# Full-height transpositions and products for the probabilities of a streaming encoder step, with a tile of its own for the prefix

## The chip, the core and the metric

The kernel runs on one core of one Trainium2 chip. The metric is the device time of one execution in microseconds (us), as the median of several runs. A core has five engines that run beside each other: TensorE (PE in the profile, with its weight loads shown apart as PEld), VectorE (DVE), ScalarE (ACT), GpSimd (POOL) and SyncE (SP). Each takes its own instructions in its own order; semaphores make one engine wait for another. DMAs are issued from an engine's queue, here from SP, and at a few places from ACT and POOL.

## The reference, cut to what matters

One layer of an encoder for 16 meta tokens and 512 prompt frames, and for 64 sample frames with 128 cached rows. Two groups of eight heads share one input projection: differential attention (two softmaxes, the second subtracted with a factor) and latent attention. Their outputs are joined and projected; a feed-forward part follows.

```
s   = einsum('bqhcd,bkhcd->bhcqk', qd, kd) * DIFF_SCALE + bias
p   = softmax(where(visible, s, neg))
p   = p[:, :, 0] - lam * p[:, :, 1]
o_d = einsum('bhqk,bkhe->bqhe', p, vd)
...
sm  = (einsum('bqhd,bkhd->bhqk', qn, km) + einsum('bqhr,bkr->bhqk', qr, krope)) * MLA_SCALE
pm  = softmax(where(visible, sm, neg))
o_m = einsum('bhqk,bkhe->bqhe', pm, vm)
```

The change touches only how `p` times the values is computed, in both groups: 16 heads in all.

## The kernel before

Matrices are held as two parts, high and low, and a product is made of three matmuls (high by high, high by low, low by high) in a 4-byte type. TensorE's order is the program's order: a small scheduler (`Streams`) interleaves generators, one for each strand of work, by estimated times, and every matmul and transposition is pinned in the order in which it was recorded. The other engines' orders are made when the program is built, from what each instruction needs.

From about 85 to 520 us the kernel projects the inputs (`project`, tile `ps`, weights `wr` split into `wh` and `wl`) and between these matmuls runs the eight differential heads (`diff_attend`). From about 520 to 785 us it runs the eight latent heads (`latent_attend`) between the matmuls of the output projection (`mix_out`, also `ps`). From there on is the feed-forward part, which the change doesn't touch.

For a head the softmax of a block of 128 queries (b = 0 to 3) is written to `pt_b[b]`, with one row for each query and one column for each key. The 64 sample queries go to `p5`. `probabilities_times_values` then works in groups g = 0 to 3. In each it turns blocks of probabilities with TensorE into the PSUM tile `tp` (L114 in the profile), ACT and DVE copy `tp` into the high and low part of `pk`, and matmuls multiply `pk` by the values into `po` (L110). Group g's matmuls (`last()`) are issued behind the transpositions of group g + 1.

Three places work with fewer than 128 rows:

- **The prefix.** The 16 meta tokens are keys of every block. To multiply high and low parts in one matmul, the three parts of their values lie stacked in rows 64 to 111 of slice 4 of `vh`; rows 0 to 63 of that slice hold the values of the 64 sample frames. For the probabilities, GpSimd copies the 16 meta columns of `pt_b[b]` three times behind its last column (`thrice`, L307, tile `p` in the profile). Group 1 transposes 112 columns of each `pt_b[b]`: the last 64 keys, which are not used, and the 48 copies. ACT copies rows 64 to 111 of `tp`, and `times_meta` multiplies 48 rows of `pk` by 48 rows of `vh`, over 512 columns, behind the transpositions of group 2.
- **The sample's probabilities.** `p5` has 64 rows. Groups 2 and 3 end with a transposition of it over 64 rows, against a 64 x 64 part of the identity.
- **The sample's products.** At the end, the tile `po5` (named `po` in the trace) gets two matmuls over 128 rows (cached values, slice 5), and two over 64 rows (own values, slice 4). The last latent head has three and three.

In the profile a TensorE row shows first the rows and columns of the stationary operand, then the rows and columns of the moving one: `48*128 48x512` is a product over 48 rows, with 512 columns streamed.

The lines of `probabilities_times_values` at these places:

```python
PE.transpose(tp[:, 384:384 + NS], p5[:, c:c + P], ident[0:NS, 0:NS])          # groups 2 and 3
PE.transpose(tp[0:STACK, b * P:(b + 1) * P], pt_b[b][:, w - NS:w + 3 * NM], ident)   # group 1
PE.matmul(po, vh[NS:STACK, 4, :], pk[NS:STACK, 1, :], start=False, stop=False)   # times_meta
```

Here NM = 16, NS = 64, STACK = 112 and P = 128.

In the latent half two heads are under way at a time, each with its own `pt_b` and `p5` (`probs[0]` for even heads, `probs[1]` for odd ones). The values of a pair of heads, `vh` and `vl`, have one buffer. When the last head's softmax is done, `tail` issues ten loads from POOL's queue: four pieces of `w_out` (`raw`, L1306) and six stored head outputs (`ml`, L1304). They are the operands of the output projection of the latent heads, the matmuls `ps<-mh,...` that begin at about 765 us.

Of the kernel before, what the change touches and what calls it, by code (L numbers as in the profile page):

```python
# [11 lines left out]
F32 = mybir.dt.float32  # L12
# [121 lines left out]
def encoder_step(  # L134
# [25 lines left out]
    def f32(ap):  # L160
        return ap.bitcast(F32)
# [65 lines left out]

    def probabilities_times_values(pt_b, p5, own0, past0, vh, vl, pool, tbanks, pso, pace, done, add=None,
                                   own_bank=True):
# [8 lines left out]
        def times_meta(pk):  # L238
            PE.matmul(po, vh[NS:STACK, 4, :], pk[NS:STACK, 1, :], start=False, stop=False)

# [8 lines left out]
        for g, blocks in enumerate((((0, 0), (0, 1), (0, 2), (0, 3)), (), ((1, 1), (1, 2), (1, 3)),  # L249
                                    ((2, 2), (2, 3), (3, 3)))):  # L250
            if g:
                yield pace
            bank, tbank = tbanks[g % len(tbanks)]
            yield from st.take(bank)
            tp = tbank()
            pk = pair(g)
            for n, (t, b) in enumerate(blocks):
                PE.transpose(tp[:, n * P:(n + 1) * P], pt_b[b][:, NM + t * P:NM + (t + 1) * P], ident)
            if g > 1:
                c = (past0, own0)[g - 2]  # L260
                PE.transpose(tp[:, 384:384 + NS], p5[:, c:c + P], ident[0:NS, 0:NS])
                kept.append(pk[:, :, 384:384 + NS])
            if g != 1:
                w = 448 if g else 512
                split(pk[:, 1, 0:w], pk[:, 0, 0:w], tp[:, 0:w])
            else:
                for b in range(4):
                    w = NM + P * (b + 1)
                    PE.transpose(tp[0:STACK, b * P:(b + 1) * P], pt_b[b][:, w - NS:w + 3 * NM], ident)
                S.activation(pk[NS:STACK, 1, :], tp[NS:STACK, :], AF.Copy)  # L270
                sub_lo(pk[96:STACK, 1, :], tp[96:STACK, :], pk[96:STACK, 1, :])
            last()
# [17 lines left out]
        if add:  # L290
            both_parts = po5[:, 0:2 * NS].rearrange("p (a b) -> p a b", a=2)
            PE.matmul(both_parts, vh[:, 5, :], kept[0], start=True, stop=False)
            PE.matmul(po5[:, NS:2 * NS], vl[:, 5, :], ph, start=False, stop=False)
            PE.matmul(po5[:, NS:2 * NS], vl[0:NS, 4, :], sh[0:NS], start=False, stop=False)
            PE.matmul(both_parts, vh[0:NS, 4, :], kept[1][0:NS], start=False, stop=True)
            done(po5[:, NS:2 * NS], SEQ, TQ)
            add(po5[:, 0:NS])
        else:
            todo = [(v[:, 5, :], p) for v, p in ((vh, ph), (vh, pl), (vl, ph))]
            todo += [(v[0:NS, 4, :], p[0:NS]) for v, p in ((vh, sh), (vh, sl), (vl, sh))]  # L300
            for n, (a, b) in enumerate(todo):
# [4 lines left out]
    def thrice(t, c0, n, copy):  # L306
        copy(t[:, n:n + 3 * NM].rearrange("p (r c) -> p r c", r=3),  # L307
             t[:, c0:c0 + NM].unsqueeze(1).to_broadcast([P, 3, NM]))
# [75 lines left out]
    with ExitStack() as ph:  # L384
# [268 lines left out]

        def keys_room(tag, name):
            return kv.tile([P, 6 * P], F32R, name=name, tag=tag, bufs=2)

        def values_room(tag, name, dtype=F32R):
            return kv.tile([P, 6, P], dtype, name=name, tag=tag, bufs=2)
# [6 lines left out]
        pt_b = [ap.tile([P, P * (b + 1) + 4 * NM], F32, name=f"p{b}") for b in range(4)]  # L665
        p5 = ap.tile([NS, NS + P], F32, name="p5")

# [62 lines left out]
        def diff_attend(h, khs, kl, vh, vl):  # L730
# [8 lines left out]
            for b in range(5):  # L739
# [3 lines left out]
                for c in range(2):  # L743
# [18 lines left out]
                    if c == 0:  # L762
# [14 lines left out]
            yield from probabilities_times_values(  # L777
                pt_b, p5, 0, NS, vh, vl, ap, [("tp", tbank)], pso, 1.0,
                lambda po, lo_, hi_: S.activation(o32[:, lo_:hi_], po, AF.Copy),
# [74 lines left out]
        def projections():  # L854
            for h in range(H):
# [34 lines left out]
                V.tensor_tensor(hv(z), ev(ps), hv(rb), op=ALU.mult)  # L890
                thrice(z, 0, T, lambda o, i: S.activation(o, i, AF.Copy))
# [4 lines left out]
                vh, vl = values_room("vh", "vh"), values_room("vl", "vl")  # L896
                nat[2 * h + 1] = st.spawn(0, values(h, z, vh, vl))
                att[h] = st.spawn(1, diff_attend(h, khs, kl, vh, vl),
# [37 lines left out]
        def query_latent(i, z):  # L936
            cqh[i], cql[i] = (zl.tile([P, TQ], F32R, name=f"cq{w}{i}", tag=f"q{i // 2}{i % 2}{t}")
                              for w, t in zip("hl", "sz"))
            if i == 0:
                sqs[0] = values_room("vl", "sqs", F32).rearrange("p a b -> p (a b)")[:, 0:TQ]  # L940
                S.activation(sqs[0], z, AF.Square)
# [63 lines left out]
        def latent_keys():  # L1005
# [4 lines left out]
            ch.extend([keys_room("kh0", "ch0"), keys_room("kh1", "ch1")])  # L1010
            cl.extend([keys_room("kl", "cl0"), values_room("vh", "cl1").rearrange("p a b -> p (a b)")])
            rk.extend([rkh, rkl])
# [7 lines left out]
            for i in range(2):  # L1020
                split(ch[i][:, 0:PROMPT], cl[i][:, 0:PROMPT], zs[4 + i][:, 0:PROMPT])
                split(ch[i][:, OWN_K:TP], cl[i][:, OWN_K:TP], zs[4 + i][:, PROMPT:T])
                split(*[x[i][:, TP:TP + 3 * NM].rearrange("p (r c) -> p r c", r=3) for x in (ch, cl)],
                      zs[4 + i][:, 0:NM].unsqueeze(1).to_broadcast([P, 3, NM]))
# [36 lines left out]
        named = dict(done=False)  # L1061
        aq, probs = [], []

        def latent_room():
# [5 lines left out]
            for i in range(2):  # L1070
                pb = [aq[0].tile([P, P * (b + 1) + 4 * NM], F32, name=f"p{b}{i}") for b in range(4)]
                p5 = aq[0].tile([NS, 2 * P], F32, name=f"p5{i}")
                G.memset(p5[:, NS + P:2 * P], 0.0)
                probs.append((pb, p5))
            for i, tag in enumerate(("vl", "vh", "vl")):
                km_rooms.append(values_room(tag, f"km{i}").rearrange("p a b -> p (a b)")[:, 0:TP])
            km_rooms.append(aq[0].tile([P, TP], F32R, name="km3"))
# [82 lines left out]
        def pair_values(j):  # L1160

            wh, wl = weights4(w_ukv4[:, :, 2 * j:2 * j + 2, 128:256], [P, 2, 2, P])
            vh = aq[0].tile([P, 6, 2 * P], F32R, name="vh")
            vl = aq[0].tile([P, 6, 2 * P], F32R, name="vl")
            for i, (o, n) in enumerate([(NM + P * j, P) for j in range(4)] + [(OWN_K, STACK), (PROMPT, PAST)]):
                yield from st.take("tp")
# [32 lines left out]
        def latent_attend(h, qn, km):  # L1199
            i = h % 2  # L1200
            pb, p5 = probs[i]
            yield 2.0
            for b in range(5):
# [9 lines left out]
                V.reciprocal(ls[0:n], ls[0:n])  # L1213
                dst = p5[:, 0:W] if b == 4 else pb[b][:, 0:W]
                V.tensor_scalar(dst, e[0:n, 0:W], ls[0:n], None, op0=ALU.mult)
                if b < 4:
                    thrice(pb[b], 0, W, G.tensor_copy)
                st.give(bank, 1.2 + 0.002 * W)
                yield 1.0
            asked[h]["done"] = True  # L1220
            yield [valued[h // 2]] + ([lat[h - 1]] if h else [])
            yield 1.5
            vh, vl = valued[h // 2]["v"]
# [5 lines left out]
            else:  # L1229
# [3 lines left out]
            yield from probabilities_times_values(  # L1233
                pb, p5, P, 0, vh[:, :, c], vl[:, :, c], aq[0], tbanks, pso, 1.0 * (h == H - 1), done, add,
                own_bank=h < H - 1)
# [866 lines left out]
```

## Time and profile before

| What | Value |
|---|---|
| Median of 3 runs | 2387.44 us (2387.34 to 2389.55) |
| Profiled execution | 2385.59 us, of which the profile's span is 2383.8 us |
| Granted TensorE clock in the profiled execution | 0.999 |
| DVE, ACT, POOL busy | 75%, 49%, 31% of the span |
| DMA | 340.92 MB moved, 143 GB/s on the mean |

The profile's busy shares are of one execution. TensorE's matmuls are pipelined, and their ends in the trace are modelled, so that the distance from one start to the next tells more than a duration. Where the trace's timeline merges equal instructions, the row has the start of the first, the time from there to the end of the last, and the count.

### The profile page before, as it was taken

The page shows a single profiled execution, that of the slowest core. Times are in us where ns is not written, and L with a number is a line of the kernel's source. Part 1 is how long each engine was busy: PE and PEld are TensorE (multiplying, and loading weights), DVE is VectorE, ACT ScalarE, POOL GpSimd, SP SyncE. Part 2 cuts the span into 40 slices and gives each one's busy share as a digit, 9 for nine tenths or more (in the row PEclk, how much of TensorE's full clock was granted, in tenths as well). Part 3 has the DMA queues.
Part 4 walks back from the last instruction along what each step waited for, and adds up shares of the span by engine and source line. Part 5 has one row for each costly group of instructions (what it writes and reads, how often), then busy time and mean ns, then how long its engine had stood idle before and what let it go on. Part 6 is the DMA issues. An engine that isn't in the chain of part 4 may idle for free.

```text
span 2383.8 us, 44654 instructions
## 1 busy us (share of the span) xinstructions
PE 2351.1 (99%) x17496; PEld 2317.2 (97%) x17496; DVE 1796.5 (75%) x2893; ACT 1163.7 (49%) x2259; POOL 727.8 (31%) x606
## 2 busy tenths in 40 slices
PE   9999999999999999999999999999999999999998
PEld 8999999999998999999999999999999999999998
DVE  6665666776665788788888888888888887877984
ACT  5554455454454554445545555555555433333444
POOL 1000000020001454554454454554554322222320
PEclk9999999999999999999999999999999999999999
DMA  9433333353323553334434434434434975655432
GB/s 286 122 90 87 86 91 92 94 162 107 95 93 126 158 163 109 127 112 150 160 115 149 161 116 147 161 119 144 161 120 149 326 258 167 228 166 169 156 103 98
DMA packets 330547, 340.92 MB, mean 143 GB/s; under 512 B 22610, under 2 KB 272376, under 8 KB 330304
## 3 DMA queue, kind: packets, MB, share of 16 engines
q1 hardware_dynamic: 328720, 334.30, 43.3%
q8 instruction: 137, 2.24, 0.4%
q0 software_dynamic: 1104, 3.22, 0.4%
q10 hardware_dynamic: 512, 0.55, 0.1%
q14 instruction: 74, 0.61, 0.1%
HBM read 267.21 MB, written 74.15 MB: 143 GB/s over the span
## 4 chain that ended last, share of the span: by engine, by line
PE 88%; DVE 5%; DMA 2%; ACT 2%; issue 2%; POOL 0%; SPq 0%; ACTq 0%; DVEq 0%; POOLq 0%
PE m L1494 38%; PE m L1498 19%; PE ps L110 19%; PE m L196 2%; PE sp L110 2%; PE po L110 2%; DVE wl L127 1%; PE tp L114 1%; PE m L1900 1%; PE pv L110 1%; PE pso L110 1%; ACT wh L127 0%; DMA wr<-in_w_in 0%; PE psv L110 0%; SPq L127 0%
## 5 line engine op out<-in xcount | busy, mean ns | idle before, releaser
L1494 PE MATMUL m<-b,wh 128*128 128x288 f32 x7168 | 1051.2, 296 | 4.5 <-DVE b L127 1.5
L1494 PEld LDWEIGHTS m<-b,wh 128*128 128x128 f32 x7168 | 982.8, 188 | 8.3 <-issue 3.3
L1498 PE MATMUL m<-b,wl 128*128 128x288 f32 x3584 | 570.0, 294 | 2.8 <-DVE wl L127 2.6
L1454 POOL TENSOR_TENSOR ws<-raw 128x512 f32<-128x512 f32 (+1 forms) x258 | 368.6, 1437 | 540.1 <-DVE wl L127 269.6
L1498 PEld LDWEIGHTS m<-b,wl 128*128 128x128 f32 x3584 | 509.1, 188 | 4.5 <-DVE wl L127 4.4
L127 ACT ACTIVATE wh<-ws 128x512 fp32r<-128x512 f32 (+1 forms) x339 | 282.9, 845 | 393.4 <-PE m L1494 245.7
L127 DVE TENSOR_TENSOR wl<-ws,wh 128x512 fp32r<-128x512 f32 (+1 forms) x339 | 379.7, 1128 | 95.4 <-ACT wh L127 92.5
L127 DVE TENSOR_TENSOR wl<-raw,wh 128x512 fp32r<-128x512 f32 (+1 forms) x393 | 367.5, 959 | 14.1 <-ACT wh L127 11.0
L127 ACT ACTIVATE wh<-raw 128x512 fp32r<-128x512 f32 (+1 forms) x393 | 231.1, 620 | 287.8 <-PE m L1494 233.3
L110 PE MATMUL ps<-xh,wh 128*128 128x296 f32 (+1 forms) x960 | 217.3, 307 | 0.5 <-ACT xh L127 0.5
L110 PE MATMUL ps<-xl,wh 128*128 128x296 f32 (+1 forms) x960 | 207.8, 298 | 0.4 <-DVE xl L127 0.3
L110 PE MATMUL ps<-xh,wl 128*128 128x296 f32 (+1 forms) x928 | 200.8, 297 | 0.5 <-DVE wl L127 0.5
L307 POOL COPY p<-p 128x48 f32<-128x48 f32 x64 | 20.2, 316 | 542.6 <-DVE p L127 500.4
L127 DVE TENSOR_TENSOR y<-y,m 128x288 f32<-128x288 f32 x280 | 125.9, 450 | 59.0 <-PE m L1498 58.8
L127 DVE TENSOR_TENSOR ws<-ws,raw 128x512 f32<-128x512 f32 (+1 forms) x129 | 112.6, 878 | 68.7 <-POOL ws L1454 66.6
L110 PEld LDWEIGHTS ps<-xh,wh 128*128 128x128 f32 x960 | 154.5, 189 | 5.6 <-issue 1.9
L110 PEld LDWEIGHTS ps<-xl,wh 128*128 128x128 f32 x960 | 154.9, 188 | 0.9 <-DVE xl L127 0.9
L110 PEld LDWEIGHTS ps<-xh,wl 128*128 128x128 f32 x928 | 150.2, 188 | 0.7 <-DVE wl L127 0.7
L127 DVE TENSOR_TENSOR wl<-wr,wh 128x1024 fp32r<-128x1024 f32 (+1 forms) x106 | 111.3, 1050 | 29.8 <-ACT wh L127 28.3
L127 ACT ACTIVATE wh<-wr 128x1024 fp32r<-128x1024 f32 (+1 forms) x108 | 97.5, 903 | 65.1 <-PE ps L110 37.3
L1719 POOL TENSOR_TENSOR c<-c,rb 128x576 f32<-128x576 f32 x42 | 67.2, 1600 | 168.4 <-ACT c L127 168.4
L127 ACT ACTIVATE parts<-c 128x1 fp32r<-128x1 f32 (+1 forms) x266 | 85.7, 322 | 33.5 <-DVE c L127 26.2
(396 smaller groups left out, 3103.6 us busy)
## 6 DMA issues: line engine op xcount, KB each, us to landing
raw<-in_ffn_w_gate SPq DMA_DIRECT2D x44, 1024.0 KB, 6.0
raw<-in_ffn_w_up SPq DMA_DIRECT2D x44, 1024.0 KB, 6.4
raw<-in_ffn_w_down SPq DMA_DIRECT2D x39, 1024.0 KB, 5.9
partspill<-parts SPq DMA_DIRECT2D x133, 288.0 KB, 2.1
b<-partspill SPq DMA_DIRECT2D x133, 288.0 KB, 6.2
wr<-in_w_in SPq DMA_DIRECT2D x54, 512.0 KB, 3.8
wr<-in_w_out SPq DMA_DIRECT2D x16, 512.0 KB, 4.1
wr<-in_w_out SPq DMA_DIRECT2D x24, 256.0 KB, 3.3
```

What stands on the lines that cost most here:

```text
L110: self.tc.keep_in_program_order(self.pe.matmul(out, lhsT, rhs, start=start, stop=stop))
L114: self.tc.keep_in_program_order(self.pe.transpose(out, in_, identity))
L127: ins = issue(*args, **kwargs)
L196: PE.matmul(outs[i], w, x[i], start=start and p == 0, stop=stop and p == 2)
L307: copy(t[:, n:n + 3 * NM].rearrange("p (r c) -> p r c", r=3), t[:, c0:c0 + NM].unsqueeze(1).to_broadcast([P, 3, NM]))
L1454: engine.tensor_tensor(w[:, k:k + m, :], pick(xs), pick(ys), op=op)
L1494: PE.matmul(banks[p], wh[k], x, start=first and new and k == 0 and x is hi, stop=False, skip_group_check=not new)
L1498: PE.matmul(banks[p], wl[k], hi, start=False, stop=last and k == n - 1, skip_group_check=not new)
L1719: engine.tensor_tensor(g[:, f, :], g[:, f, :], rb2, op=ALU.mult)
L1900: PE.matmul(bank[:, c0:c0 + 256], a[:, o:o + n], b, start=k + i == 0, stop=k == len(acts) - 1 and i == 2)
```

## The change

Every transposition and product of the three places gets 128 rows; the rows that are added hold zeros.

- The three copies of the meta columns go to a tile `pm` of their own (128 x 4 x 128, columns 64 to 111 of each block), which is set to zero once by POOL. Group 1 transposes `pm[:, b, :]`, all 128 columns, and ACT evicts all 128 rows. `pt_b` loses its 48 extra columns.
- `p5` gets 128 rows and 256 columns, zeroed once: columns 0 to 127 for the cached keys, 128 to 191 for the own ones. Its transpositions run over 128 rows against the whole identity, and stream 128 columns instead of 64. In the differential heads the write to `p5` becomes two instructions on DVE.
- Rows 96 to 127 of slice 4 of `vh` and rows 64 to 127 of slice 4 of `vl` are zeroed by POOL for each differential head and each pair of latent heads (`clear_rest`). The products on slice 4 take all 128 rows.
- In the latent half there is one `pm` for both sets of probabilities. So the copies into it are recorded not within the softmax loop, but behind it and behind the wait for the head before (`lat[h - 1]`).

The core of the diff:

```diff
         def times_meta(pk):
-            PE.matmul(po, vh[NS:STACK, 4, :], pk[NS:STACK, 1, :], start=False, stop=False)
+            PE.matmul(po, vh[:, 4, :], pk[:, 1, :], start=False, stop=False)
...
             if g > 1:
-                c = (past0, own0)[g - 2]
-                PE.transpose(tp[:, 384:384 + NS], p5[:, c:c + P], ident[0:NS, 0:NS])
+                PE.transpose(tp[:, 384:512], p5[:, (g - 2) * P:(g - 1) * P], ident)
...
                 for b in range(4):
-                    w = NM + P * (b + 1)
-                    PE.transpose(tp[0:STACK, b * P:(b + 1) * P], pt_b[b][:, w - NS:w + 3 * NM], ident)
-                S.activation(pk[NS:STACK, 1, :], tp[NS:STACK, :], AF.Copy)
-                sub_lo(pk[96:STACK, 1, :], tp[96:STACK, :], pk[96:STACK, 1, :])
+                    PE.transpose(tp[:, b * P:(b + 1) * P], pm[:, b, :], ident)
+                S.activation(pk[:, 1, :], tp, AF.Copy)
+                sub_lo(pk[96:P, 1, :], tp[96:P, :], pk[96:P, 1, :])
...
-            PE.matmul(po5[:, NS:2 * NS], vl[0:NS, 4, :], sh[0:NS], start=False, stop=False)
-            PE.matmul(both_parts, vh[0:NS, 4, :], kept[1][0:NS], start=False, stop=True)
+            PE.matmul(po5[:, NS:2 * NS], vl[:, 4, :], sh, start=False, stop=False)
+            PE.matmul(both_parts, vh[:, 4, :], kept[1], start=False, stop=True)
...
-            todo += [(v[0:NS, 4, :], p[0:NS]) for v, p in ((vh, sh), (vh, sl), (vl, sh))]
+            todo += [(v[:, 4, :], p) for v, p in ((vh, sh), (vh, sl), (vl, sh))]
...
+    def clear_rest(vh, vl):
+        G.memset(f32(vh[96:P]), 0.0)
+        G.memset(f32(vl[NS:P]), 0.0)
...
+        def probability_tiles(pool, i=""):
+            pt_b = [pool.tile([P, P * (b + 1) + NM], F32, name=f"p{b}{i}") for b in range(4)]
+            p5 = pool.tile([P, 2 * P], F32, name=f"p5{i}")
+            G.memset(p5, 0.0)
+            return pt_b, p5
+
+        def prefix_tile(pool):
+            pm = pool.tile([P, 4, P], F32, name="pm")
+            G.memset(pm, 0.0)
+            return pm
...
-                dst = p5 if b == 4 else pt_b[b][:, 0:W]
-                V.scalar_tensor_tensor(dst, es[0][0:n, 0:W], ls[0:n, 0:1], es[1][0:n, 0:W],
-                                       op0=ALU.mult, op1=ALU.subtract)
+                for dst, k in [(pt_b[b][:, 0:W], slice(0, W))] if b < 4 else [
+                        (p5[0:NS, P:P + NS], slice(0, NS)), (p5[0:NS, 0:P], slice(NS, W))]:
+                    V.scalar_tensor_tensor(dst, es[0][0:n, k], ls[0:n, 0:1], es[1][0:n, k],
+                                           op0=ALU.mult, op1=ALU.subtract)
                 if b < 4:
-                    thrice(pt_b[b], 0, W, G.tensor_copy)
+                    repeat(pm[:, b, NS:NS + 3 * NM], pt_b[b][:, 0:NM], G.tensor_copy)
...
             asked[h]["done"] = True
             yield [valued[h // 2]] + ([lat[h - 1]] if h else [])
+            for b in range(4):
+                repeat(pm[:, b, NS:NS + 3 * NM], pb[b][:, 0:NM], G.tensor_copy)
             yield 1.5
```

The remaining lines rename rooms and pass `pm` along. `repeat` is `thrice` with its destination given.

TensorE's order doesn't change: instruction stands beside instruction, only the shapes differ. Here is a piece of the difference on PE in the first differential head, group 2: the transpositions of `pt_b[2]` and `pt_b[3]` (`p_909`, `p_910`), that of `p5` (`p_911`), and the product with the prefix behind it. Printed is the shape of the result, which doesn't show the rows that are summed over.

```order
 L114 MATMUL tp<-ident,p_909 128x128
 L114 MATMUL tp<-ident,p_910 128x128
-L114 MATMUL tp<-ident,p_911 128x64
-L110 MATMUL po<-pk_1570,vh 128x512
+L114 MATMUL tp<-ident,p_911 128x128
+L110 MATMUL po<-pk_1578,vh 128x512
 L110 MATMUL ps<-xh_116,wh 128x288 x2
```

Nothing has moved there: the transposition of `p5` writes 128 columns in place of 64, and the product stands where it stood.

GpSimd's order does change in the latent half. Here is POOL at the end of it, before: the four copies of the last head (`p_6120` to `p_6123`), then the loads that `tail` issues (`raw`, `ml`).

```order
L307 COPY p_6120<-p_6120 128x48
L307 COPY p_6121<-p_6121 128x48
L307 COPY p_6122<-p_6122 128x48
L307 COPY p_6123<-p_6123 128x48
L1306 DMA raw<-in_w_out 128x4x128 x4
L1304 DMA ml_9034<-mspill_78 128x576
```

And the same place in the changed kernel, with the last copy of head 6 (`p_6144`) and the four of head 7 (`p_6147` to `p_6150`):

```order
L315 MEMSET vh 32x256
L306 COPY pm<-p_6144 128x48
L306 COPY pm<-p_6147 128x48
L306 COPY pm<-p_6148 128x48
L306 COPY pm<-p_6149 128x48
L306 COPY pm<-p_6150 128x48
L1323 DMA raw<-in_w_out 128x4x128 x4
L1321 DMA ml_9071<-mspill_78 128x576
```

The order of names is the same, but the four copies of head 7 now write the one `pm`. So each of them waits until the transposition of the same block of head 6 has read it, and the ten loads stand behind them.

More of the change, by code (lines that the diff above doesn't have):

```diff
@@ L226, in project_stacked, with probabilities_times_values @@
                 yield 0
-    def probabilities_times_values(pt_b, p5, own0, past0, vh, vl, pool, tbanks, pso, pace, done, add=None,
+    def probabilities_times_values(pt_b, pm, p5, vh, vl, pool, tbanks, pso, pace, done, add=None,
                                    own_bank=True):
@@ L304, in probabilities_times_values, with repeat @@
         st.give("po", 1.0)
-    def thrice(t, c0, n, copy):
-        copy(t[:, n:n + 3 * NM].rearrange("p (r c) -> p r c", r=3),
-             t[:, c0:c0 + NM].unsqueeze(1).to_broadcast([P, 3, NM]))
+    def repeat(dst, src, copy):
+        n = dst.shape[1] // NM
+        copy(dst.rearrange("p (r c) -> p r c", r=n), src.unsqueeze(1).to_broadcast([P, n, NM]))
     def stacked_values(vh, vl, src):
@@ L652, in encoder_step, with flat_room, values_room @@
         zk = zk_cm.__enter__()
[L654 to L658, printed above, removed]
+        ROOM = TP + 3 * NM
+        def flat_room(tag, name, dtype=F32R):
+            return kv.tile([P, ROOM], dtype, name=name, tag=tag, bufs=2)
+        keys_room = flat_room
+        def values_room(tag, name):
+            return flat_room(tag, name)[:, 0:6 * P].rearrange("p (a b) -> p a b", a=6)
         qs = [[[zl.tile([P, TQ], F32R, name=f"q{i}{c}{s}", tag=f"q{i}{c}{s}") for s in "sz"] for c in range(2)]
@@ L664, in encoder_step @@
                 G.memset(f32(qs[i][c][1][both[1 - c], :]), 0.0)
-        pt_b = [ap.tile([P, P * (b + 1) + 4 * NM], F32, name=f"p{b}") for b in range(4)]
-        p5 = ap.tile([NS, NS + P], F32, name="p5")
+        def probability_tiles(pool, i=""):
[7 more added lines that the diff above has]
+            return pm
+        (pt_b, p5), pm = probability_tiles(ap), prefix_tile(ap)
         def natural(src32, c0, rest, dst_p, stores, keep):
@@ L777, in diff_attend @@
             yield from probabilities_times_values(
-                pt_b, p5, 0, NS, vh, vl, ap, [("tp", tbank)], pso, 1.0,
+                pt_b, pm, p5, vh, vl, ap, [("tp", tbank)], pso, 1.0,
                 lambda po, lo_, hi_: S.activation(o32[:, lo_:hi_], po, AF.Copy),
@@ L890, in projections @@
                 V.tensor_tensor(hv(z), ev(ps), hv(rb), op=ALU.mult)
-                thrice(z, 0, T, lambda o, i: S.activation(o, i, AF.Copy))
+                repeat(z[:, T:T + 3 * NM], z[:, 0:NM], lambda o, i: S.activation(o, i, AF.Copy))
                 if h == 0:
@@ L896, in projections @@
                 vh, vl = values_room("vh", "vh"), values_room("vl", "vl")
+                clear_rest(vh[:, 4, :], vl[:, 4, :])
                 nat[2 * h + 1] = st.spawn(0, values(h, z, vh, vl))
@@ L939, in query_latent @@
             if i == 0:
-                sqs[0] = values_room("vl", "sqs", F32).rearrange("p a b -> p (a b)")[:, 0:TQ]
+                sqs[0] = flat_room("vl", "sqs", F32)[:, 0:TQ]
                 S.activation(sqs[0], z, AF.Square)
@@ L1010, in latent_keys @@
             ch.extend([keys_room("kh0", "ch0"), keys_room("kh1", "ch1")])
-            cl.extend([keys_room("kl", "cl0"), values_room("vh", "cl1").rearrange("p a b -> p (a b)")])
+            cl.extend([keys_room("kl", "cl0"), flat_room("vh", "cl1")])
             rk.extend([rkh, rkl])
@@ L1022, in latent_keys @@
                 split(ch[i][:, OWN_K:TP], cl[i][:, OWN_K:TP], zs[4 + i][:, PROMPT:T])
-                split(*[x[i][:, TP:TP + 3 * NM].rearrange("p (r c) -> p r c", r=3) for x in (ch, cl)],
+                split(*[x[i][:, TP:ROOM].rearrange("p (r c) -> p r c", r=3) for x in (ch, cl)],
                       zs[4 + i][:, 0:NM].unsqueeze(1).to_broadcast([P, 3, NM]))
@@ L1061, in encoder_step @@
         named = dict(done=False)
-        aq, probs = [], []
+        aq, probs, prefix = [], [], []
         def latent_room():
@@ L1070, in latent_room @@
             for i in range(2):
[L1071 to L1074, printed above, removed]
+                probs.append(probability_tiles(aq[0], i))
+            prefix.append(prefix_tile(aq[0]))
             for i, tag in enumerate(("vl", "vh", "vl")):
-                km_rooms.append(values_room(tag, f"km{i}").rearrange("p a b -> p (a b)")[:, 0:TP])
+                km_rooms.append(flat_room(tag, f"km{i}")[:, 0:TP])
             km_rooms.append(aq[0].tile([P, TP], F32R, name="km3"))
@@ L1164, in pair_values @@
             vl = aq[0].tile([P, 6, 2 * P], F32R, name="vl")
+            clear_rest(vh[:, 4, :], vl[:, 4, :])
             for i, (o, n) in enumerate([(NM + P * j, P) for j in range(4)] + [(OWN_K, STACK), (PROMPT, PAST)]):
@@ L1200, in latent_attend @@
             i = h % 2
-            pb, p5 = probs[i]
+            (pb, p5), pm = probs[i], prefix[0]
             yield 2.0
@@ L1213, in latent_attend @@
                 V.reciprocal(ls[0:n], ls[0:n])
-                dst = p5[:, 0:W] if b == 4 else pb[b][:, 0:W]
+                dst = p5[0:NS, 0:W] if b == 4 else pb[b][:, 0:W]
                 V.tensor_scalar(dst, e[0:n, 0:W], ls[0:n], None, op0=ALU.mult)
-                if b < 4:
-                    thrice(pb[b], 0, W, G.tensor_copy)
                 st.give(bank, 1.2 + 0.002 * W)
@@ L1233, in latent_attend @@
             yield from probabilities_times_values(
-                pb, p5, P, 0, vh[:, :, c], vl[:, :, c], aq[0], tbanks, pso, 1.0 * (h == H - 1), done, add,
+                pb, pm, p5, vh[:, :, c], vl[:, :, c], aq[0], tbanks, pso, 1.0 * (h == H - 1), done, add,
                 own_bank=h < H - 1)
```

## The prediction

> **What bounds the kernel now.** I read first the page, then the table by stage, then TensorE's waits in the stage that the change touches.
>
> ```profile
> span 2383.8 us, 44654 instructions
> PE 2351.1 (99%) x17496; PEld 2317.2 (97%) x17496; DVE 1796.5 (75%) x2893; ACT 1163.7 (49%) x2259; POOL 727.8 (31%) x606
> ...
> PE 88%; DVE 5%; DMA 2%; ACT 2%; issue 2%; POOL 0%; SPq 0%; ACTq 0%; DVEq 0%; POOLq 0%
> ...
> 85.00:520.00 435.00, 431.65 (x3138) 419.70 (x3137) 284.87 (x602) 216.71 (x444) 27.96 (x48) 1.00 0.35 98
> 560.00:785.00 225.00, 216.97 (x1568) 205.98 (x1568) 132.94 (x266) 106.32 (x221) 18.47 (x43) 1.00 0.32 100
> ...
> PE tp L114 <- DVE pk L127: 2.1, 4, 0.7
> ```
>
> TensorE is busy 99% of the span, and 88% of the chain that ended last runs through it. In the two stages where the heads run (the columns behind the length are PE, PEld, DVE, ACT, POOL) it is idle 3.35 of 435 us and 8.03 of 225 us; DVE works 65% and 59% of the time. So what TensorE saves there is saved in the end, except next to one of its few waits; the last row is one of the longest, 2.1 us in four waits.
>
> But busy is not the same as at full pace. The weight loads show it:
>
> ```profile
> L114 PEld LDWEIGHTS tp<-ident,p 64*128 64x128 f32 x32 | 4.3, 136 | 5.3 <-issue 5.3
> ```
>
> These are the 32 transpositions of `p5`, two for each head: ahead of each stands a pause of 5.3 / 32 = 0.17 us, for which no semaphore accounts.
>
> **The change part by part.** All steps are read from TensorE's starts in the first differential head.
>
> *A: the end of group 2, `times_meta`, and the matmuls behind it.* First the place, then the place in group 1 where everything has 128 rows:
>
> ```profile
> 119.62 0.69 PE L114 MATMUL tp<-ident,p 128*128 128x128 f32 x4
> 120.05 0.49 PE L110 MATMUL po<-pk,vh 48*128 48x512 f32 x1
> 120.47 0.54 PE L110 MATMUL ps<-xh,wh 128*128 128x288 f32 x2
> 120.84 0.43 PE L110 MATMUL ps<-xl,wh 128*128 128x288 f32 x2
> ...
> 116.11 0.60 PE L114 MATMUL tp<-ident,p 128*112 128x128 f32 x4
> 116.46 0.47 PE L110 MATMUL po<-pk,vh 128*128 128x512 f32 x1
> 116.77 0.40 PE L110 MATMUL po<-pk,vl 128*128 128x512 f32 x1
> ...
> 117.24 0.42 PE L110 MATMUL ps<-xh,wh 128*128 128x288 f32 x2
> 117.50 0.43 PE L110 MATMUL ps<-xl,wh 128*128 128x288 f32 x2
> ```
>
> Four transpositions take 0.43 us with the 64-row one among them, and 0.35 without. The 512 columns take 0.42 over 48 rows, and 0.31 over 128. The next pair of matmuls takes 0.37, and 0.26 in the reference. Together 1.22 against 0.92: 0.30 us a head. The reference has the wider transposition (128 columns in place of 64) in it.
>
> *B: the end of group 3 and the values' product behind it.*
>
> ```profile
> 122.97 0.69 PE L114 MATMUL tp<-ident,p 128*128 128x128 f32 x4
> 123.58 0.44 PE L110 MATMUL po<-pk,vh 128*128 128x384 f32 x1
> 123.86 0.34 PE L110 MATMUL po<-pk,vl 128*128 128x384 f32 x1
> ```
>
> 0.61 for the four, 0.28 for the product: 0.89. By the reference 0.35, and 0.31 less what 128 columns take; two products of 512 columns go from 116.77 to 117.24, so 128 columns take 0.06. That makes 0.60, and 0.29 us a head.
>
> *C: the sample's products.* The place, then short products and their end elsewhere with 128 rows:
>
> ```profile
> 128.24 0.47 PE L110 MATMUL po<-pk,vl 128*128 128x64 f32 x2
> 128.55 0.30 PE L110 MATMUL po<-pk,vh 64*128 64x128 f32 x1
> 128.78 0.54 PE L110 MATMUL ps<-xh,wh 128*128 128x296 f32 x2
> 129.16 0.43 PE L110 MATMUL ps<-xl,wh 128*128 128x296 f32 x2
> ...
> 126.50 0.49 PE L110 MATMUL ps<-xh,wh 128*128 128x296 f32 x2
> 126.82 0.44 PE L110 MATMUL ps<-xl,wh 128*128 128x296 f32 x2
> ...
> 778.45 0.30 PE L110 MATMUL po<-pk,vh 128*128 128x64 f32 x2
> 778.59 0.28 PE L110 MATMUL po<-pk,vl 128*128 128x64 f32 x1
> ```
>
> Now 0.92 us from 128.24 to 129.16. No row shows exactly this sequence with 128 rows. Two 64-column products took 0.14 in the last head; at most they go at the pace of four transpositions, 0.35 / 4 = 0.09 each, or 0.18. The product of 128 columns then takes 0.06 to 0.11, and the pair behind short products 0.32 (126.50), or 0.26 as behind long ones. Bounds 0.46 to 0.61; I take 0.61, since 0.32 was measured behind short products: 0.31 us a head.
>
> **Sum on TensorE:** 0.30 + 0.29 + 0.31 = 0.90 us a head, 14.4 us for 16.
>
> *What is taken back.* Where TensorE waits for an eviction, only what starts the eviction earlier counts.
>
> ```profile
> 589.82 0.75 PE L114 MATMUL tp<-ident,p 128*128 128x128 f32 x4 [0.59 <-DVE pk L127]
> ...
> L127 ACT ACTIVATE pk<-tp x64: 528/564/602, 108.6 to 774.1; 128x448 fp32r<-128x448 f32 x32, 128x512 fp32r<-128x512 f32 x16, 48x512 fp32r<-48x512 f32 x16
> L127 DVE TENSOR_TENSOR pk<-tp,pk x64: 617/655/698, 109.3 to 774.6; 128x448 fp32r<-128x448 f32 x32, 128x512 fp32r<-128x512 f32 x16, 16x512 fp32r<-16x512 f32 x16
> ```
>
> Three of the four waits for `pk` stand, like this one, between A and B of a latent head: of A's 0.30 only the transpositions' 0.08 counts there, minus 0.22 each, 0.7 us. At the end of head 6 TensorE waits for ACT (below), and about 0.2 of C goes the same way. The evictions themselves keep their price: 48 or 128 rows lie within 528 to 602 ns on ACT, 16 rows or 128 within 617 to 698 on DVE.
>
> *What is added elsewhere.* The split write to `p5` is eight more DVE instructions, each shorter than the 0.65 us above; DVE's idle third hides them. POOL gets 27 more memsets:
>
> ```profile
> L1073 POOL MEMSET p<- x2: 145/146/147, 522.7 to 522.7; 64x64 f32 x2
> L307 POOL COPY p<-p x64: 224/224/1171, 88.5 to 746.5; 128x48 f32<-128x48 f32 x64
> ```
>
> Each of the 24 small ones has 128 or 256 columns where this one has 64, so about 0.15 to 0.6 us. POOL works 28 of 435 us and 18 of 225, and would cost something only if a memset stood in its queue ahead of copies that TensorE waits for. The memsets wait for the last product of an earlier head, which is over before the next copies have their softmax. The copies are as many as before. Odd latent heads get theirs only when the even head's transpositions are through: four copies of at most 1.17 us, and between the transpositions of heads 6 and 7 (751.73 and 768.06, below) there are 16 us. I cost all this at nothing.
>
> *The loads at the end.* POOL's last four copies now wait for group 1 of head 6:
>
> ```profile
> 747.20 3.06 POOL L1306 DMA_DIRECT2D raw<-in_w_out  x4 [0.51 <-DMA xo<-xspill]
> 750.25 3.21 POOL L1304 DMA_DIRECT2D ml<-mspill  x6
> ...
> 751.73 0.60 PE L114 MATMUL tp<-ident,p 128*112 128x128 f32 x4
> ...
> 768.06 0.60 PE L114 MATMUL tp<-ident,p 128*112 128x128 f32 x4
> ...
> 764.57 0.62 ACT L127 ACTIVATE rows<-raw 128x512 fp32r<-128x512 f32 x1
> 765.09 0.67 ACT L127 ACTIVATE mh<-ml 128x576 fp32r<-128x576 f32 x1
> ...
> ml<-mspill POOLq DMA_DIRECT2D x6, 288.0 KB, 5.8
> ```
>
> The ten issues begin not at 747.2 but behind the transpositions (752.3) and four copies, at about 753.4, and the first `ml` at 756.4. With 5.8 us to landing it is there at 762.2; ACT asks for it at 765.09, or 0.9 earlier by the saving in head 6. Some 2 us are left, so this too costs nothing.
>
> **Result:** 14.4 - 0.7 - 0.2 = 13.5 us. The profiled execution took 2385.59 us, the span and 1.8 around it; it would take 2372.1. The median of before lies 1.85 above it: 2374.0.
>
> **Two rules weighed.** The pauses above are 0.17 us ahead of each 64-row transposition, and 0.06 to 0.11 on the far side. The Trainium skill, TensorEngine Tiling (Array Packing), Key Properties, says that changing the tiling mode drains TensorE. By that rule the pauses go with the partial rows, and the trace agrees in that a pause stands at each switch (0.17 us). A second page speaks against the change:
>
> ```profile
> 120.05 0.27 PE L114 MATMUL tp<-ident,p 64*128 64x64 f32 x1
> ```
>
> The 64-row transposition (rows 0 to 63) starts at 120.05, with the product with the prefix (rows 64 to 111, first fence of A). The Trainium skill, TensorE: Matmul & The Clock Gate, Part 3, says that matmuls on different row groups run concurrently; its table of recommendations says that a small-K matmul takes as long as one with K = 128. By that rule the change loses the overlap and gains nothing, and the sum would be that of the second rival, 2.4 us more, where by the first rule it is 13.5 us less. The trace agrees as to the overlap (0.00 us between the starts); it weighs less there than the pauses.
>
> **Rivals.**
>
> 1. *TensorE runs into evictions in the latent half.* For it: 8.03 us of idle time there, against 3.35 in the first half. If every latent head lost A but for 0.08, and C altogether, it would gain 0.08 + 0.29 = 0.37, and all 16 gain 8 x 0.90 + 8 x 0.37 = 10.2 us: 2377.3. Against it: only four waits for `pk`.
> 2. *The pauses stay,* because they belong to the order of transposition and product and not to the number of rows. Then the change only loses the overlap, one step of 0.09 us, and streams two wider transpositions (64 columns more, 0.03 each by the 0.06 of 128): 0.15 x 16 = 2.4 us more, 2389.8. Against it: group 1 has the same order without a pause (116.11 to 116.77).
> 3. *Slower: the loads behind POOL's copies.* ACT takes `raw` and `ml` in order, TensorE's `ps<-mh` waits for it, and each us of delay past the 2 us of slack is a us of the whole. The gain is gone when the first `ml` lands 15.5 us later than reckoned, and from 20 us on the kernel is slower by over 0.2%: 2392.5 at 20.5. Against it: a load lands in 5.8 us.
>
> **How the numbers follow.** The forecast, 2374.0, gets 0.74. Rival 1 gets 0.13, rival 2 gets 0.08, rival 3 gets 0.03; 0.02 are for a larger gain, with C at its lower bound (0.46) and nothing taken back: 0.30 + 0.29 + 0.46 = 1.05, 16.8 us, 2370.6. The range goes from there to 2379.0, past rival 1. A difference of 0.2%, 4.8 us, is about what a measurement of this kernel can tell from none. Faster: 0.74 + 0.13 + 0.02 = 0.89; rival 2 lies within 0.2%, 0.08; slower 0.03.
>
> **What would show it.** In the profile after, the steps at A, B and C should be 0.92, 0.60 and 0.61 us, with no idle time by "issue" ahead of the transpositions of `p5`. The stages from 85 to 785 us should end about 13 us earlier, and the stage behind keep its length. A wait of `ps` for `mh` of over 2 us at the end of the latent half would speak for rival 3, longer waits of `tp` and `po` for rival 1. Unchanged steps at A and B would make the prediction wrong.

## The result, and the profile after

| | before | after |
|---|---|---|
| Median of 6 runs each on one chip | 2388.78 us (2387.34 to 2390.82) | 2374.78 us (2372.94 to 2379.6) |
| Profiled execution, and its span | 2385.59 us, 2383.8 us | 2373.83 us, 2372.1 us |

The ratio is 0.9948, with a 95% interval of 0.9936 to 0.9959: faster, by 14.0 us in the medians and 11.8 us between the profiled executions. The forecast was 2374.0 us.

These lines of the page and of the table by stage after the change stand against those of before (columns behind the length: PE, PEld, DVE, ACT, POOL, granted clock, DMA share, GB/s):

```profile
PE 2340.2 (99%) x17496; PEld 2317.7 (98%) x17496; DVE 1795.5 (76%) x2901; ACT 1162.4 (49%) x2259; POOL 733.7 (31%) x633
...
85.00:520.00 435.00, 431.20 (x3178) 424.40 (x3178) 288.17 (x615) 218.38 (x448) 32.22 (x65) 1.00 0.35 100
560.00:785.00 225.00, 216.51 (x1607) 210.87 (x1607) 138.17 (x273) 112.27 (x233) 25.11 (x54) 1.00 0.33 103
```

TensorE has as many instructions as before and is busy as much; the same stretch of time now holds some 40 more matmuls in each stage (3178 and 1607, from 3138 and 1568). Nothing became idle instead: the idle time is 3.80 and 8.49 us, from 3.35 and 8.03.

The weight loads of the transpositions, in the table of groups by shape, show where the pauses went:

```profile
L114 PEld LDWEIGHTS tp<-ident,p 128*128 128x128 f32 x192 | 23.1, 140 | 4.2 <-DVE pk L127 3.2 <-issue 0.9
L114 PEld LDWEIGHTS tp<-ident,pm 128*128 128x128 f32 x64 | 7.7, 141 | 0.4 <-issue 0.3
```

The 32 loads over 64 rows, which had 5.3 us of "issue" ahead of them, are now in the first row, with 0.9 us for all 192. The timeline of TensorE at the three places of the first head:

```profile
120.04 0.60 PE L114 MATMUL tp<-ident,p 128*128 128x128 f32 x4
120.40 0.48 PE L110 MATMUL po<-pk,vh 128*128 128x512 f32 x1
120.71 0.42 PE L110 MATMUL ps<-xh,wh 128*128 128x288 f32 x2
120.97 0.43 PE L110 MATMUL ps<-xl,wh 128*128 128x288 f32 x2
...
123.09 0.60 PE L114 MATMUL tp<-ident,p 128*128 128x128 f32 x4
123.45 0.42 PE L110 MATMUL po<-pk,vh 128*128 128x384 f32 x1
123.71 0.34 PE L110 MATMUL po<-pk,vl 128*128 128x384 f32 x1
...
128.09 0.35 PE L110 MATMUL po<-pk,vl 128*128 128x64 f32 x2
128.27 0.31 PE L110 MATMUL po<-pk,vh 128*128 128x128 f32 x1
128.42 0.48 PE L110 MATMUL ps<-xh,wh 128*128 128x296 f32 x2
128.74 0.43 PE L110 MATMUL ps<-xl,wh 128*128 128x296 f32 x2
```

From start to start, place A takes 0.93 us (120.04 to 120.97), B 0.62 (123.09 to 123.71), C 0.65 (128.09 to 128.74). The means over the 16 heads, from the starts of the same instructions in both traces, are:

| Place | before, us | after, us | difference | forecast |
|---|---|---|---|---|
| A, group 2 and the product with the prefix | 1.221 | 0.936 | -0.285 | -0.30 |
| B, group 3 | 0.915 | 0.625 | -0.290 | -0.29 |
| C, the sample's products | 0.909 | 0.654 | -0.255 | -0.31 |

That is 0.83 us a head, 13.3 us for 16. Yet from the first matmul after 85 us to the same matmul before 790 us of the trace before, the kernel is only 11.2 us shorter (704.80 and 693.56 us). So 2.0 us were given back between the three places.

### The profile page after: what moved, and what is told of

Read it like the earlier page. It is cut to its first block, busy times and chain, and to the rows that moved or that the text cites. A ratio compares the mean times of both kernels' runs of the same rounds, so it can differ in the third digit from the quotient of the medians.

```text
span 2372.1 us, 44701 instructions
## 1 busy us (share of the span) xinstructions
PE 2340.2 (99%) x17496; PEld 2317.7 (98%) x17496; DVE 1795.5 (76%) x2901; ACT 1162.4 (49%) x2259; POOL 733.7 (31%) x633
## 5 line engine op out<-in xcount | busy, mean ns | idle before, releaser
L306 POOL COPY pm<-p 128x48 f32<-128x48 f32 x64 | 19.8, 321 | 354.0 <-DVE p L127 304.4
```

What stands on the lines that cost most here:

```text
L306: copy(dst.rearrange("p (r c) -> p r c", r=n), src.unsqueeze(1).to_broadcast([P, n, NM]))
```

## The experiments

In the tables below, A, B and C are means over 16 heads, as above. "Stage" is the time between the same two matmuls, at 85 and 790 us before. Whole times vary from run to run (the kernel before took 2373.06 to 2390.26 us in the 31 runs beside the first four kernels here), so the small effects are read from the trace. The ratios, with 95% intervals, are worked out from all the runs and can differ a little from the quotient of the medians.

**1 to 3. The parts alone.** The first kernel keeps the wide p5 transpositions and takes the rest back:

```diff
 # against the changed kernel
-            PE.matmul(po, vh[:, 4, :], pk[:, 1, :], start=False, stop=False)
+            PE.matmul(po, vh[NS:STACK, 4, :], pk[NS:STACK, 1, :], start=False, stop=False)
...
-            PE.matmul(po5[:, NS:2 * NS], vl[:, 4, :], sh, start=False, stop=False)
-            PE.matmul(both_parts, vh[:, 4, :], kept[1], start=False, stop=True)
+            PE.matmul(po5[:, NS:2 * NS], vl[0:NS, 4, :], sh[0:NS], start=False, stop=False)
+            PE.matmul(both_parts, vh[0:NS, 4, :], kept[1][0:NS], start=False, stop=True)
...
```

The last head's products on slice 4 go back to `0:NS` as well.

> The p5 transpositions keep 128 rows; the product with the prefix goes back to 48 rows and the sample's products on slice 4 to 64. Steps on TensorE, mean of 16 heads, were A 1.221, B 0.915, C 0.909 us before the change and 0.936, 0.625, 0.654 after it. Theory 1, a pause stands at each passage between an instruction of 64 rows or fewer and one of 128, whatever the two compute: B falls as after the change (0.625), since its only partial instruction is gone; A gains next to nothing (1.19), since the product over 48 rows alone still has a passage on either side; C stays at 0.909. Together 16 x (0.03 + 0.29) = 5.2 us less than before. Theory 2, the pause belongs to the 64-row transposition alone (its own start): A would fall by about half of its gain too (1.08) and B by all, together 6.9 us. Theory 3, the pauses belong to the order transposition, then product: nothing changes, or it loses the overlap, 0 to 2.4 us more than before.

The second has the wide product with the prefix alone, the third the wide sample's products alone; both put this line back:

```diff
-                PE.transpose(tp[:, 384:512], p5[:, (g - 2) * P:(g - 1) * P], ident)
+                PE.transpose(tp[:, 384:384 + NS], p5[0:NS, (g - 2) * P:(g - 1) * P], ident[0:NS, 0:NS])
```

> Only the product with the prefix gets 128 rows; the p5 transpositions and the sample's products keep 64. Theory 1 (a pause at each passage between partial and full rows): the 64-row transposition still has a passage on either side, so A keeps its pauses and gains only what the far side of the product had, about 0.14 (1.085 us); B and C as before the change (0.915, 0.909). Together 2.2 us less than before. Theory 2 (the pause belongs to the 64-row transposition alone): A 1.22, nothing gained, 0 us. A rival on the overlap (partial instructions on different rows run beside each other, and the product loses that): A up by 0.09 to 0.31 us, 1.4 to 5.0 us more than before. If the parts are independent, this gain and that of the run before (p5 alone) add up at A to 0.285; by theory 1 they add up to only 0.17, because the two partial instructions of A shared their passages.

> Only the sample's products get 128 rows; p5 transpositions and the product with the prefix stay partial. Theory 1: C 0.654 us as after the change, A and B as before it (1.221, 0.915), 16 x 0.255 = 4.1 us less than before. Rival, C's gain needs the other parts (for example because the matmuls behind it came at another time): C 0.90, 0 us.

| Full rows in | A | B | C | A, B and C, 16 heads | stage | median (before: 2385.94) and ratio |
|---|---|---|---|---|---|---|
| p5 transpositions | 1.324 | 0.625 | 0.908 | -3.0 us | -2.5 us | 2384.23; 0.9994 (0.9979 to 1.001) |
| product with the prefix | 1.224 | 0.914 | 0.907 | 0.0 | +1.9 | 2385.91; 1.0008 (0.9992 to 1.0023) |
| sample's products | 1.218 | 0.917 | 0.655 | -4.1 | -1.8 | 2383.22; 1.0 (0.9984 to 1.0016) |
| all three (first run of after) | 0.936 | 0.625 | 0.654 | -13.3 | -11.2 | above |

The whole times don't separate such small parts; the steps do. B and C follow theory 1 and do not depend on the other parts. A does not follow the expectations. With the p5 transposition alone it got **0.10 us worse** than before (1.19 was expected), and with the product alone it gained nothing (1.085 was expected). The second theory's 1.22 fits the second run but not the first (1.08). Only both together give 0.285. Here are TensorE and its weight loads at A in the first of these kernels:

```profile
119.49 0.60 PE L114 MATMUL tp<-ident,p 128*128 128x128 f32 x4
120.02 0.49 PE L110 MATMUL po<-pk,vh 48*128 48x512 f32 x1
120.44 0.54 PE L110 MATMUL ps<-xh,wh 128*128 128x288 f32 x2
120.81 0.43 PE L110 MATMUL ps<-xl,wh 128*128 128x288 f32 x2
...
120.02 0.18 PEld L110 LDWEIGHTS po<-pk,vh 48*128 48x128 f32 x1 [0.17 <-issue]
120.44 0.30 PEld L110 LDWEIGHTS ps<-xh,wh 128*128 128x128 f32 x2 [0.24 <-issue]
```

and the weight loads at A after the whole change:

```profile
120.37 0.19 PEld L110 LDWEIGHTS po<-pk,vh 128*128 128x128 f32 x1
120.48 0.42 PEld L110 LDWEIGHTS ps<-xh,wh 128*128 128x128 f32 x2
```

After the change the load for `ps` starts at 120.48, 0.23 us ahead of its matmul (120.71), while the product with the prefix still streams. In the experiment the load for `ps` starts together with its matmul at 120.44: it isn't brought forward past the change from 48 rows to 128. The same holds on the near side, where load and product both start at 120.02. Whether the late load makes the price, or only goes with it, these rows don't show. The pause has simply moved: the table of groups shows it ahead of the 48-row product, where it was ahead of the p5 transposition before.

```profile
L110 PEld LDWEIGHTS po<-pk,vh 48*128 48x128 f32 x16 | 2.9, 183 | 2.7 <-issue 2.7
```

In the second kernel the transposition over 64 rows keeps its pause, and the product over 128 rows behind it starts 0.20 us later, not beside it:

```profile
119.30 0.69 PE L114 MATMUL tp<-ident,p 128*128 128x128 f32 x4
119.92 0.50 PE L110 MATMUL po<-pk,vh 128*128 128x512 f32 x1
...
119.72 0.14 PEld L114 LDWEIGHTS tp<-ident,p 64*128 64x128 f32 x1 [0.17 <-issue]
```

So the price belongs to an excursion from 128 rows to few and back. Against the 0.936 of full rows, an excursion of the transposition alone costs 0.29 us (1.224), of the 48-row product alone 0.39 (1.324), and of both together 0.285 (1.221). Two partial instructions that stand together cost no more than one.

**4. Rows between 64 and 128.** The changed kernel with 96 and 112 rows in place of 128:

```diff
-            PE.matmul(po, vh[:, 4, :], pk[:, 1, :], start=False, stop=False)
+            PE.matmul(po, vh[0:STACK, 4, :], pk[0:STACK, 1, :], start=False, stop=False)
...
-                PE.transpose(tp[:, 384:512], p5[:, (g - 2) * P:(g - 1) * P], ident)
+                PE.transpose(tp[:, 384:480], p5[0:96, (g - 2) * P:(g - 1) * P], ident[0:96, 0:96])
```

The products on slice 4 at C take `0:STACK` as well.

> The kernel after the change, but with 96 rows in the p5 transpositions (96 columns streamed) and 112 rows in the product with the prefix and in the sample's products. Theory 1a, what counts is more than 64 rows against 64 or fewer: A, B, C as after the change (0.936, 0.625, 0.654; the transposition up to 0.02 shorter), the time that of after within 1 us. Theory 1b, what counts is any row short of 128: the pauses return, A about 1.2, B about 0.9, C about 0.9, and the time is that of before.

A, B and C were 0.939, 0.627 and 0.655 us, the median 2375.89 us (ratio 0.9965, 0.9948 to 0.9981). TensorE at A, in its timeline:

```profile
120.06 0.57 PE L114 MATMUL tp<-ident,p 128*128 128x128 f32 x4
120.42 0.48 PE L110 MATMUL po<-pk,vh 112*128 112x512 f32 x1
120.73 0.43 PE L110 MATMUL ps<-xh,wh 128*128 128x288 f32 x2
```

No pause: 96 and 112 rows go as 128 do (the row with x4 has the shape of its first; the last of the four has 96 rows). It isn't the unused rows that cost, but falling to 64 or fewer. Where the limit lies between 64 and 96, and whether the first row matters (64 for the product over 48 rows, 0 for all the others), was not tried.

**5. The same instructions in another order.** In the kernel before, the second and third product of the sample change places in 15 heads, so that 128, 64, 128 and 64 rows follow each other:

```diff
             PE.matmul(both_parts, vh[:, 5, :], kept[0], start=True, stop=False)
-            PE.matmul(po5[:, NS:2 * NS], vl[:, 5, :], ph, start=False, stop=False)
             PE.matmul(po5[:, NS:2 * NS], vl[0:NS, 4, :], sh[0:NS], start=False, stop=False)
+            PE.matmul(po5[:, NS:2 * NS], vl[:, 5, :], ph, start=False, stop=False)
```

> The kernel before the change, with the same instructions, but in the sample's products the second and third change places: 128, 64, 128, 64 rows instead of 128, 128, 64, 64 (15 heads; the last one keeps its order). Theory (the price is paid for each passage into partial rows and out again, not for each instruction): C grows by one more passage in and out, 0.255 us by C's own, up to 0.385 by that of the product over 48 rows alone: 1.16 to 1.29 us a head, 3.8 to 5.8 us more in all. Rival (each partial instruction has its own price): C stays at 0.909 us, and the time at that of before. A and B stay at 1.221 and 0.915 by both.

The timeline of TensorE in the first head:

```profile
128.64 0.22 PE L110 MATMUL po<-pk,vh 128*128 128x128 f32 x1
128.79 0.52 PE L110 MATMUL po<-pk,vl 64*128 64x64 f32 x2
129.24 0.33 PE L110 MATMUL po<-pk,vh 64*128 64x128 f32 x1
129.49 0.54 PE L110 MATMUL ps<-xh,wh 128*128 128x296 f32 x2
129.88 0.29 PE L110 MATMUL ps<-xl,wh 128*128 128x296 f32 x1
```

From the first product to the second pair of `ps` there were 0.97 us before (128.19 to 129.16), and now 1.24 (128.64 to 129.88). The mean of the 15 heads grew by 0.26 us: 0.093 ahead of the first 64-row product, 0.166 behind it. By this 3.9 us of the stage's growth of 4.6 are accounted for. The median was 2392.79 us against 2386.84, ratio 1.0024 (1.0015 to 1.0033). Not one instruction was added: the rival, a price for each partial instruction, falls.

**6. The changed kernel again, and with more distance between the groups.** First the changed kernel once more.

> The changed kernel once more, on the same chip as the next two, to have a time and a profile beside them: steps at A, B and C 0.936, 0.625 and 0.654 us again; of the 13.3 us saved at these places about 2 us given back elsewhere between 85 and 790 us, at the same places as in the first profile (two products of `po` with the low part of `pk` in heads 1 and 4, 0.25 us each; the wait of `tp` for `pk` in latent head 0; the wait of `sp` for `nm`, 0.25 and 0.13 us). What only a passing low clock made would stand elsewhere this time.

It took 2378.74 us in the median (before: 2386.84; ratio 0.9963, 0.995 to 0.9977). So the whole gained 8.1 us here, 5.5 to 11.9 by the interval, where it had been 14.0, 9.8 to 15.3. The stage repeats far better, and its gain lies in both intervals. The steps were 0.936, 0.625 and 0.654 us, the stage 11.3 us shorter, and 2.0 us were given back again. The held-up `po` products of heads 1 and 4, the wait of `tp` in latent head 0 (0.29 us) and the first wait of `sp` (0.26) came back; the second wait of `sp` did not (below 0.06). Then the same kernel with more distance:

```diff
-            st.give(bank, 1.9)
-        yield max(pace, 0.8)
+            st.give(bank, 2.2)
+        yield max(pace, 1.2)
```

> The changed kernel with more distance between the groups of a head: the planner gives the bank of `tp` back after 2.2 instead of 1.9 of its time units, and waits 1.2 instead of 0.8 ahead of the last group, so that other matmuls stand between an eviction and its use. Theory (what was given back are waits for evictions that TensorE now reaches too early): the products of `po` with the low part of `pk` are no longer held up in heads 1 and 4 and in the odd latent heads (0.25, 0.25 and three times 0.11 us), the stage from 85 to 790 us is up to 1 us shorter than in the changed kernel, and the whole up to 1 us. Rival (every wait that goes is replaced by one elsewhere, since the order of all the work shifts): the waits move, and the stage stays within 0.5 us, or grows by up to 2 us.

It took 2379.2 us, and the stage was 6.0 us longer than in the changed kernel. From the last matmul of the second pass of `po` to the first of the third there are 0.06 us where nothing holds it up. In the latent heads it was that in all eight, as the theory has it; in the differential heads the third pass was late in heads 0 and 3 instead (0.21 us each) and, with 1.01 us, in head 7. The longest waits were others too. The first of these two the changed kernel doesn't have among its longest, the second was 1.2 us there:

```profile
PE ps L110 <- DVE z L127: 1.9, 1, 1.9
PE pv L110 <- DVE vh L127: 1.7, 1, 1.7
```

The rival holds: distance moves the waits and adds some. Its upper bound of 2 us was too low; a lowered clock accounts for 3.4 us of the 6 (last section). No version was faster than the changed kernel. The one with 96 and 112 rows (ratio 0.9965) can't be told from it (0.9948 and 0.9963).

## Why the prediction was right

**The mechanism, TensorE's pauses at partial rows: shown.** The forecast's sum took each place as a whole, from a place with 128 rows throughout, and A and B came out within 0.015 us. Experiment 5 shows that the price hangs on the passage, experiment 4 that it goes without filling all 128 rows.

**The split of A: not known at the time.** The working of A lists four transpositions (0.08), the product (0.11) and the pair behind (0.11), which reads as if each had its own gain. The runs show that these are one excursion, and half a change would have gained nothing or lost 0.10 us.

**C was mis-sized:** 0.255 us in place of 0.31, 0.9 us in all. The term that failed is the product of 128 columns, put at 0.06 to 0.11 us by longer streams and transpositions. It took 0.144 (to the next start at 128.42 above, 0.15 by the rounded rows). The two 64-column products, reckoned at 0.18, took 0.19, and the pair was as reckoned. These products make 0.04 of the 0.055 us a head; the rest is that the mean of the place before was 0.909, not the 0.92 of the first head.

**What is taken back was mis-sized, and in another place:** 2.0 us in place of 0.9. The wait of `tp` for `pk` between A and B changed by +0.27 us in latent head 0, +0.09 in head 4, -0.24 in head 2: nearly nothing on the sum, where 0.7 was forecast. The step that failed is that only waits which exist already would eat gains. New ones came, above all where the third pass of `po` needs the low part of `pk`. In the timelines of head 1, before, DVE ended it at 177.34 and TensorE came to it at 177.54:

```profile
176.72 0.62 DVE L127 TENSOR_TENSOR pk<-tp,pk 128x448 fp32r<-128x448 f32 x1 [0.29 <-ACT pk L127]
...
177.14 0.34 PE L110 MATMUL po<-pk,vh 128*128 128x256 f32 x2
177.31 0.39 PE L110 MATMUL po<-pk,vl 128*128 128x256 f32 x2
177.54 0.40 PE L110 MATMUL po<-pk,vh 128*128 128x256 f32 x2
```

After:

```profile
175.54 0.55 ACT L127 ACTIVATE pk<-tp 128x448 fp32r<-128x448 f32 x1
...
176.12 0.62 DVE L127 TENSOR_TENSOR pk<-tp,pk 128x448 fp32r<-128x448 f32 x1 [0.38 <-ACT pk L127]
...
176.15 0.44 PE L110 MATMUL po<-pk,vh 128*128 128x256 f32 x2
176.43 0.39 PE L110 MATMUL po<-pk,vl 128*128 128x256 f32 x2
176.80 0.45 PE L110 MATMUL po<-pk,vh 128*128 128x256 f32 x2
```

DVE ends at 176.74, TensorE goes on at 176.80. It came 0.23 us from the pass before (176.43 + 0.23, as between 177.31 and 177.54) and stood for 0.14. The first pass, which reads what ACT ended at 176.09, lost another 0.11 (0.28 us to the second pass, where it had been 0.17). Heads 1 and 4 gave back 0.25 us each in this way, three latent heads 0.11 each, the waits of `sp` for `nm` 0.25 and 0.13, that of `ps` for `mh` 0.13, and several others under 0.1. The kernels with parts of the change bear it out: with the low clock taken off (last section), the kernel with 0 us gained at its places gave back about 0.2 us, those with 3.0 and 4.1 gave back 0.5 and 0.6, those with 13.2 and 13.3 gave back 2.5 and 2.0. What is given back grows with the gain; it is not a price of the new tiles, copies and memsets, which all these kernels have. That longer distances would win it back was the theory of experiment 6, and it fell there for the kernel as a whole.

**The final number** hit closer than its parts, and that was luck. The stage gained 11.2 us, not 13.5. The start added 0.4, the feed-forward stage took off 0.9 (1593.95 and 1593.07 us from the stage's end), which makes the 11.8 of the profiled executions. The median lies 0.95 us above the profiled execution, not 1.85 as before, which made up for half of the 1.7 us by which the forecast of the profiled execution (2372.1) was too low. Against its own base, 2387.44 us from three runs, the forecast was 13.4 us less. That lies in the interval of the first comparison (9.8 to 15.3), but above that of the repetition (5.5 to 11.9): the mechanism repeats, the close hit doesn't.

**Rival 1** (TensorE runs into evictions in the latent half) did not come true at the places that it named: A and C kept their gains in all latent heads. What evictions took back is in the 2.0 us above. **Rival 2** (the pauses belong to the order) falls by A and B, but what speaks for it is true in part: the overlap of the two partial instructions was worth having, as the first experiment shows, which lost it. The Trainium skill, TensorE: Matmul & The Clock Gate, Part 3, says that matmuls on different row groups run concurrently. The trace of before agrees (0.00 us between the starts), and with one of the two widened A is 0.10 us slower or the same. The Trainium skill, TensorEngine Tiling (Array Packing), Key Properties, says that a change of tiling mode drains TensorE, without a price; here it is 0.26 to 0.39 us for going and coming back.

**Rival 3** (the loads behind POOL's copies): the timelines of POOL and of ACT after the change, and the last row from the table of DMA issues (count, KB each, median us to landing):

```profile
742.70 0.72 POOL L306 COPY pm<-p 128x48 f32<-128x48 f32 x4 [21.59 <-PE tp L114]
743.85 3.06 POOL L1323 DMA_DIRECT2D raw<-in_w_out  x4 [0.42 <-ACT pk L127]
746.90 3.21 POOL L1321 DMA_DIRECT2D ml<-mspill  x6
...
755.01 0.67 ACT L127 ACTIVATE mh<-ml 128x576 fp32r<-128x576 f32 x1
...
ml<-mspill POOLq DMA_DIRECT2D x7, 288.0 KB, 6.2
```

As forecast, the issues wait for the transpositions of head 6 and the copies. The first `ml` would be there at 746.9 + 6.2 = 753.1 by the median, and ACT takes it at 755.01 when its other work is through: 1.9 us of slack, where 2 were reckoned. (By its own landing in the trace, 751.92, it is 3.1 us.) The wait of `ps` for `mh` grew from 0.82 to 0.94 us, not by over 2. A kernel with the copies back in the softmax loop was not tried.

## What to carry to other kernels

In a stream of 128-row matmuls, count the excursions to 64 rows or fewer, not the partial instructions: each costs 0.26 to 0.39 us here, and 128 rows with zeros, or 96 rows, go without that price. Widen all the partial instructions that stand together or none of them, since half of a pair gained nothing or lost. On an engine that is 99% busy, look also for results that arrive just in time now: in head 1 a margin of 0.2 us turned into a wait of 0.14, and waits for other engines, new ones and longer ones, are most of the 2.0 us that came off the 13.3.

## What was not expected of the hardware

**The price has a far side, larger than the near one.** Going from a full transposition to a 64-row one cost 0.094 us (0.203 between starts, not 0.109). Going back from it to a full product cost 0.174 (0.202, where full to full takes 0.028) and 0.02 behind it. From a full transposition to the 48-row product it was 0.174 as well, and back 0.108 and 0.105 at the next two starts. The idle time by "issue" of the weight loads doesn't show all of it: it stands ahead of the partial instruction, and again behind the 48-row product (0.24 us in the first experiment above), but there is none behind the 64-row transposition of B.

**Half the clock for a few us, in the middle of busy stages.** The table by short windows in the second experiment (the product with the prefix alone), the clock third from the end:

```profile
766.00:768.00 2.00, 1.71 (x9) 1.48 (x9) 2.00 (x4) 1.32 (x3) 0.00 (x0) 0.76 1.07 332
768.00:770.00 2.00, 2.00 (x10) 1.98 (x9) 0.42 (x1) 0.05 (x1) 0.54 (x1) 0.50 0.94 226
770.00:772.00 2.00, 2.00 (x13) 1.82 (x13) 1.39 (x3) 1.70 (x3) 0.00 (x0) 0.89 1.00 343
```

The granted clock fell to 0.50, matmuls that otherwise start 0.13 us apart started 0.24 apart, and 2 x (0.24 + 0.50 + 0.11) = 1.7 us were lost: nearly all the 1.9 us by which this stage was longer than before. The third experiment lost as much at 742 to 746 us (0.57 in two such windows, 4 x 0.43 = 1.7), and the kernel with more distance had two such stretches:

```profile
494.00:498.00 4.00, 2.41 (x17) 2.18 (x16) 2.28 (x3) 1.42 (x3) 0.00 (x0) 0.92 0.40 108
498.00:502.00 4.00, 4.00 (x23) 4.00 (x22) 2.33 (x6) 1.75 (x5) 1.47 (x1) 0.65 0.68 223
...
760.00:764.00 4.00, 4.00 (x18) 3.51 (x18) 2.04 (x4) 1.74 (x3) 0.54 (x1) 0.57 0.93 279
```

4 x (0.08 + 0.35 + 0.43) = 3.4 us in these rows. In the first of them TensorE was idle for 1.6 us. The Trainium skill, TensorE: Matmul & The Clock Gate, Part 1, has the clock at half after an idle window of about 3.4 us; these gaps are shorter. Before and after the change the same stages held 1.00 with waits of up to 1.3 us, so an idle gap of this size doesn't decide it alone.

The clock records in the traces add something. There are six such drops in the nine traces (apart from one at the end of every kernel), the two others in the feed-forward part of the first and the fourth experiment (from 1872.6 and 1861.7 us). Each lasts 3.41 us at 0.50, hence the 1.7 us, and begins a whole number of 3.4133 us behind the moment from which the record has the full clock (761.17 us = 223 x 3.4133 in the second experiment, 1856.85 us = 544 x 3.4133 in the fourth). In the 3.41 us ahead of each, TensorE was busy only 0.40 to 0.67 of the time. But one such stretch with 0.49, in the kernel with more distance from 736.3 us, had no drop behind it. So where a gap lies on this grid of 3.41 us may matter beside its length; what decides stays open.
